# Attention scores from a doubled high query and stacked high and low keys, with unread transfers and transposes added at the end

## The chip, the core and the metric

The kernel runs on one core of a Trainium2 chip. The core has a matrix engine (TensorE, PE in the profile, with its weight loads as PEld), three engines for elementwise work (VectorE is DVE, ScalarE is ACT, GpSimd is POOL) and a sync engine (SP) that issues most transfers. The metric is the device time of one execution in microseconds (us). The kernel before took 609.4 us, the median of three runs (609.2 to 609.53).

## The reference

Two layers of a decoder trunk work on x of 256 x 1024 float32. In each layer one normalised input goes through one wide projection (9808 columns); three causal attentions of 8 heads of 64 read their queries, keys and values from it:

```
h = rms_norm(x, gain)
proj = einsum('bsd,de->bse', h, w_in)
oa = moba_attention(rope(qa), rope(ka), va) * silu(ga)     # mixer a
ob = dsa_attention(rope(qb), rope(kb), vb, qi, ki, wi) * silu(gb)   # mixer b
oc = forgetting_attention(qc, kc, vc, log_f) * silu(gc)    # mixer c
y = einsum('nbsw,nwd->bsnd', stack([oa, ob, oc]), w_branch)
x + einsum('bsd,de->bse', sum(sigmoid(merge) * y), w_out)
```

With 256 positions mixer a is plain causal attention (one block). Mixer b keeps, for each query, 64 keys by an index score: the weighted sum over 8 index heads of relu(qi . ki), with one key shared by the 8 heads. A last rms_norm follows the two layers.

## The kernel before

All products of float32 numbers on PE are made from split operands. ScalarE writes a high part in the matmul's own format (float32r), VectorE writes the low part as the difference, and a product is the sum of three matmuls: high by high, low by high, high by low. For weights this is `piece` (high on L362, low on L366); the activations `hTh` and `hTl` are split once a layer.

A unit is one output tile of the input projection: 24 matmuls with 256 moving columns for 128 output channels (`unit_b`, recorded at L410 in `mm_ops`), into one of three PSUM tiles called `proj`. Two heads of a mixer make a pair, and a pair is a unit each for query, gate and key. A query of mixer a or b is rotated (`rope`: VectorE, GpSimd, VectorE, GpSimd) and split into `qh` and `ql` by `split_to` (L396 and L397); a query of mixer c is split straight from PSUM (L400 and L401). A key is written by `write_bd` into a pair of tiles `bd..h` and `bd..l` of two blocks each: block 0 has head 0 in partitions 0 to 63, block 1 has head 1 in partitions 64 to 127, and the rest was set to zero at the start. So one matmul over 128 partitions with 2n moving columns gives n scores of each of the two heads, their columns alternating. `scores` (L584 to L586) issues six matmuls: for queries 0 to 127 against 128 keys three of 256 columns into `s0`, for queries 128 to 255 against 256 keys three of 512 columns into `s1`. Each has its own weight load, since the query part is the stationary operand.

`attend` goes on from there: VectorE adds mask or bias and takes the extreme (L647), ScalarE takes the exponential (L651), PE transposes the normalised rows (L673), the result is split again and multiplied with the values (L690 to L693, two of these with 128 moving columns), and `gated` multiplies with the gate. `index_scores` does query, scores, relu (L792, L793) and the weighted sum `isc` (L801, L803) for the four pairs of index heads; its key is written once a layer by `ev_kwf`, the same rows into both blocks.

A layer calls `scores` 16 times: four index pairs, and four pairs each of mixers a, c and b, in this order. Between them stand the merge gates (`unit_m`) and the branch projections (`unit_y`), interleaved by `between`; after mixer b come the rest of them and the output projection, two row tiles by two halves (and for the last layer the last tile in two column parts). `final_part` and `final_norm` then scale a row tile into `tmp6` and send it out, 384 columns by ScalarE's queue (L570) and 640 by SP's (L571).

The order of the instructions on each engine is fixed when the program is built: every operation is handed to a planner with its engine, an assumed duration, what it reads and writes, and a key. The planner simulates the engines and takes, on the engine that can start next, the operation with the smallest key. An operation marked `port` isn't planned on VectorE while one is planned on GpSimd. On the chip each engine runs its list in order and waits on semaphores.

Of the kernel before, what the change touches and what calls it, by code (L numbers as in the profile page):

```python
# [15 lines left out]
S = 256  # L16
# [31 lines left out]
NB1 = 0  # L48
# [186 lines left out]
def hybrid_trunk(ctx, tc, x, norm_gain, w_in, forget_bias, w_branch, w_out, final_gain, consts, out):  # L235
# [46 lines left out]
    qs = [[pool.tile([128, S], F32R, name=f"q{p}{i}") for i in range(3)] for p in "hl"]  # L282
# [8 lines left out]
    bd = [[pool.tile([128, 2, S], F32R, name=f"bd{i}{p}") for p in "hl"] for i in range(NBD)]  # L291
# [41 lines left out]
    for nm, n, cols, dt in (("rsh", 2, S, F32), ("rr", 2, S, F32),  # L333
                            ("th", 2, S, F32), ("g", 4, S, F32), ("e", 4, 384, F32), ("st", 8, 8, F32),
                            ("fb", 2, 384, F32), ("ot", 2, S, F32), ("t8", 4, 8, F32), ("mth", MTH, S, F32)):
        tag(nm, n, [128, cols], dt)
# [134 lines left out]
    def new_bd():  # L471

        b = Buf("bd")
        return b, [[Tok(), Tok()], [Tok(), Tok()]]


# [97 lines left out]
    def scores(q, k, ktoks, key):  # L574
        s0, s1 = Buf("s"), Buf("s")
        kt = [t for h in ktoks for t in h]

        def go():
            qh, ql = T(q[0]), T(q[1])
            kh, kl = T(k)  # L580
            for o, sl, n in ((T(s0)[:, :256], slice(0, 128), 128), (T(s1), slice(128, 256), 256)):
                o = o.rearrange("p (c h) -> p c h", h=2)
                mh, ml = (x[:, :, :n].rearrange("p h c -> p c h") for x in (kh, kl))
                PE.matmul(o, qh[:, sl], mh, start=True, stop=False)  # L584
                PE.matmul(o, ql[:, sl], mh, start=False, stop=False)  # L585
                PE.matmul(o, qh[:, sl], ml, start=False, stop=True)  # L586
        pe(go, 3 * (t_mm(256) + t_mm(512)), [q[0], q[1], k] + kt, [s0, s1], key, "qk", MARGIN)
        return s0, s1

    class Pair:  # L590
# [3 lines left out]
        def ev_q(self, ps, key):  # L594
            q = self.q = (Buf("qh"), Buf("ql"))
            if self.mixer == "c":
                split_to(lambda: plain(T(q[0])), lambda: plain(T(q[1])), lambda: tiles(T(ps)[:, :S]), S, True, [ps], q[0], q[1],
                         key, -0.125, "q")
            else:
                r = rope(ps, "q", key)  # L600
                split_to(lambda: plain(T(q[0])), lambda: plain(T(q[1])), lambda: tiles(T(r)), S, False, [r], q[0], q[1], key, name="q")

        def ev_k(self, ps, key):
            self.k, self.kt = new_bd()
            src = ps if self.mixer == "c" else rope(ps, "k", key)
            write_bd(src, self.k, self.kt, key, self.mixer == "c")
# [30 lines left out]
        def attend(self, key):  # L637
            bs = [self.bias(h, key) for h in range(2)]
            s0, s1 = scores(self.q, self.k, self.kt, key)
            es, ke = [], []  # L640
            for h in range(2):
# [4 lines left out]
                for t, a, n, s in parts:  # L646
                    dve(lambda t=t, a=a, n=n, s=s, e=e, st=st, b=b, h=h: DVE.tensor_tensor_reduce(  # L647
                        T(e)[:, a:a + n], T(s)[:, :2 * n].rearrange("p (c h) -> p h c", h=2)[:, h], b()[:, a:a + n], 1.0, 3e38, ALU.add, ALU.min,
# [72 lines left out]
    def write_bd(src, b, toks, key, ps, shared=False):  # L721
        for h in range(2):
            o = slice(64 * h, 64 * h + 64)
            s = (lambda: tiles(T(src)[0:64, :S])) if shared else (lambda o=o: tiles(T(src)[o, :S]))
            hi = lambda o=o, h=h: plain(T(b)[0][o, h])
            lo = lambda o=o, h=h: plain(T(b)[1][o, h])
            act(lambda hi=hi, s=s: ACT.activation(hi(), s(), AF.Copy), S, ps, [src, k_bdz], [toks[h][0]], key, "bd", HALF + (0.0 if ps else 104.0), touch=[b])
            dve(lambda hi=hi, lo=lo, s=s: DVE.tensor_tensor(lo(), s(), hi().bitcast(F32), op=ALU.subtract), S,
                [src, toks[h][0]], [toks[h][1]], key, "bd", t_dve(S) + HALF + 15.0, touch=[b], port=not ps)


    def ev_kwf(l, ps, key):
        act(lambda: ACT.activation(plain(wf[64:80]), tiles(T(ps)[64:80, :S]), AF.Copy), S, True, [ps], [k_wf], key, "wf")
        b, toks = new_bd()
        write_bd(rope(ps, "k", key, 64), b, toks, key, False, shared=True)
        return b, toks
# [357 lines left out]
```

## Time and profile before

| | before |
|---|---|
| median of three runs | 609.4 us |
| profiled execution, its own time | 609.16 us |
| its span in the profile | 607.4 us |
| PE busy | 599.1 us (99%) |
| PEld busy | 580.8 us (96%) |
| DVE busy | 537.9 us (89%) |
| ACT busy | 406.8 us (67%) |
| POOL busy | 85.7 us (14%) |
| bytes moved | 105.55 MB, mean 174 GB/s |

The time of an execution holds the span of the profile and what lies around it, here 609.16 - 607.4 = 1.76 us. Matmuls are pipelined, so a busy PE says only that matmuls follow one another; the pitch of their starts tells what one costs. L12 in a row is line 12 of the kernel; `out<-in` names the tiles an instruction writes and reads.

### The profile page before, as it was taken

Reading aid. Unit: us, or ns where it says so; the run is one execution under the profiler, and the core shown is the slowest. Engines: PE = TensorE matmul, PEld = TensorE weight load, DVE = VectorE, ACT = ScalarE, POOL = GpSimd, SP = SyncE. Lnnn points to the kernel's source line nnn. Section 1 sums busy time; section 2 is a strip of 40 time slices with the busy share of each in tenths; the row PEclk is TensorE's granted clock in tenths of the full one; section 3 lists DMA queues with packets and bytes.
Section 4 is the critical chain, followed back from the end, with each engine's and each line's share of the span. In section 5 each row is a group of like instructions: output and inputs, shape, how many; then the busy total and the mean of one; then the engine's idle time right before and its main releaser. Section 6 shows DMA issues by size and latency. Waiting matters only on the chain.

```text
span 607.4 us, 12561 instructions
## 1 busy us (share of the span) xinstructions
PE 599.1 (99%) x4856; PEld 580.8 (96%) x4856; DVE 537.9 (89%) x1270; ACT 406.8 (67%) x811; POOL 85.7 (14%) x100
## 2 busy tenths in 40 slices
PE   9999999999999999999999999999999999999995
PEld 8999999999999999999889999999999999999995
DVE  8799999887998999999588899978889989999883
ACT  6775487685776766785587554957767675859741
POOL 1224021100000222200003311201000004230001
PEclk9999999999999999999999999999999999999998
DMA  9866455837372562666555637474464437355801
GB/s 304 255 209 208 127 169 157 278 104 231 117 245 70 159 203 92 209 211 206 161 181 169 206 102 246 139 219 142 153 187 174 141 115 224 109 182 164 280 35 70
DMA packets 93853, 105.55 MB, mean 174 GB/s; under 512 B 4321, under 2 KB 82401, under 8 KB 93793
## 3 DMA queue, kind: packets, MB, share of 16 engines
q1 hardware_dynamic: 93504, 104.36, 53.8%
q8 instruction: 38, 0.62, 0.4%
q10 hardware_dynamic: 288, 0.39, 0.2%
q14 instruction: 23, 0.18, 0.1%
HBM read 103.69 MB, written 1.05 MB: 172 GB/s over the span
## 4 chain that ended last, share of the span: by engine, by line
PE 88%; DVE 9%; issue 1%; ACT 1%; DMA 0%; POOL 0%; POOLq 0%; DVEq 0%
PE proj L410 74%; DVE wl L366 3%; PE t L673 3%; PE proj L970 2%; PE s L586 2%; PE s L585 2%; PE s L584 2%; PE o L690 1%; PE o L693 1%; DVE isc L824 1%; DVE t L823 1%; PE t L629 1%; DVE isc L803 1%; DVE rsh L465 1%; PE o L692 0%
## 5 line engine op out<-in xcount | busy, mean ns | idle before, releaser
L366 DVE TENSOR_TENSOR wl<-raw,wh 128x1024 fp32r<-128x1024 f32 (+1 forms) x190 | 237.1, 1257 | 24.2 <-ACT wh L362 22.6
L362 ACT ACTIVATE wh<-raw 128x1024 fp32r<-128x1024 f32 (+1 forms) x190 | 198.6, 1058 | 74.3 <-PE proj L410 43.1
L410 PE MATMUL proj<-hTh,wh 128*128 128x256 f32 (+1 forms) x1040 | 246.4, 276 | 0.0
L410 PE MATMUL proj<-hTl,wh 128*128 128x256 f32 (+1 forms) x1040 | 245.6, 275 | 0.0
L410 PEld LDWEIGHTS proj<-hTl,wh 128*128 128x128 f32 (+1 forms) x1040 | 199.0, 191 | 0.4
L410 PEld LDWEIGHTS proj<-hTh,wh 128*128 128x128 f32 (+1 forms) x1040 | 198.9, 191 | 0.4
L410 PE MATMUL proj<-hTh,wl 128*128 128x256 f32 (+1 forms) x1040 | 160.1, 276 | 0.0
L410 PEld LDWEIGHTS proj<-hTh,wl 128*128 128x128 f32 (+1 forms) x1040 | 138.0, 191 | 0.9
L466 POOL TENSOR_TENSOR rsh<-rsh,cst 128x256 f32<-128x256 f32 (+1 forms) x42 | 33.0, 786 | 343.0 <-DVE rsh L465 333.9
L651 ACT ACTIVATE e<-e,st 128x128 f32<-128x128 f32 x96 | 42.6, 446 | 9.2 <-DVE st L647 8.9
L468 POOL TENSOR_TENSOR rr<-rr,rsh 128x256 f32<-128x256 f32 (+1 forms) x42 | 44.4, 1059 | 9.7 <-ACT wh L362 3.4
L410 PE MATMUL proj<-wh,v 128*128 128x512 f32 (+1 forms) x144 | 33.7, 356 | 0.0
L410 PE MATMUL proj<-og0l,wh 128*128 128x256 f32 x128 | 31.9, 275 | 0.0
L410 PE MATMUL proj<-og0h,wh 128*128 128x256 f32 x128 | 31.9, 275 | 0.0
L410 PE MATMUL proj<-wh,hTh 128*128 128x512 f32 x80 | 31.4, 393 | 0.0
L410 PE MATMUL proj<-wh,hTl 128*128 128x512 f32 x80 | 30.5, 382 | 0.2 <-DVE hTl L532 0.2
L706 ACT ACTIVATE ot<-o 64x256 f32<-64x256 f32 x48 | 18.3, 381 | 16.8 <-PE o L693 16.3
L410 PEld LDWEIGHTS proj<-wh,v 128*128 128x128 f32 x144 | 25.2, 190 | 2.9
L678 DVE TENSOR_TENSOR ptl<-t,pth 128x384 fp32r<-128x384 f32 x48 | 25.1, 551 | 0.2
L410 PE MATMUL proj<-og0h,wl 128*128 128x256 f32 x128 | 24.7, 275 | 0.0
L410 PEld LDWEIGHTS proj<-og0h,wh 128*128 128x128 f32 x128 | 24.6, 192 | 0.0
L410 PEld LDWEIGHTS proj<-og0l,wh 128*128 128x128 f32 x128 | 24.6, 192 | 0.0
(194 smaller groups left out, 1012.3 us busy)
## 6 DMA issues: line engine op xcount, KB each, us to landing
raw<-in_w_in_dram SPq DMA_DIRECT2D x74, 1024.0 KB, 5.2
raw<-in_w_branch_dram SPq DMA_DIRECT2D x24, 512.0 KB, 3.9
raw<-in_w_out_dram SPq DMA_DIRECT2D x8, 1024.0 KB, 5.5
raw<-in_w_in_dram SPq DMA_DIRECT2D x3, 512.0 KB, 6.3
x<-in_x_dram SPq DMA_DIRECT2D x4, 256.0 KB, 4.1
raw<-in_w_in_dram SPq DMA_DIRECT2D x2, 320.0 KB, 6.7
out_dram<-tmp SPq DMA_DIRECT2D x2, 320.0 KB, 2.5
raw<-in_w_in_dram SPq DMA_DIRECT2D x2, 256.0 KB, 3.4
```

Of the source, the lines that this page charges most:

```text
L362: ACT.activation(p[0].v, sel(c.v), AF.Copy)
L366: DVE.tensor_tensor(p[1].v, sel(c.v), p[0].v.bitcast(F32), op=ALU.subtract)
L410: PE.matmul(o(), a(), b(), start=first and i == 0, stop=last and i == n - 1)
L466: gps(lambda: POOL.tensor_tensor(T(sh)[:np_], T(sh)[:np_], s[:np_], op=ALU.mult), S, [k_rope], [sh], key, "rope")
L468: gps(lambda: POOL.tensor_tensor(T(r)[:np_], T(r)[:np_], T(sh)[:np_], op=ALU.add), S, [sh], [r], key, "rope")
L584: PE.matmul(o, qh[:, sl], mh, start=True, stop=False)
L585: PE.matmul(o, ql[:, sl], mh, start=False, stop=False)
L586: PE.matmul(o, qh[:, sl], ml, start=False, stop=True)
L651: act(lambda t=t, a=a, n=n, e=e, st=st: ACT.activation(T(e)[:, a:a + n], T(e)[:, a:a + n], AF.Exp, bias=T(st)[:, t:t + 1], scale=-1.0, acc ...
L673: PE.transpose(T(ps)[:, i * 128:(i + 1) * 128], T(es[h])[:, i * 128:(i + 1) * 128], ident)
L678: dve(lambda h=h, src=src: DVE.tensor_tensor(T(pl)[:, h], src(), T(ph)[:, h].bitcast(F32), op=ALU.subtract), 384, [ps, kp[h][0]], [kp[h][1 ...
L706: act(lambda r=r, h=h: ACT.activation(T(t)[r], T(o)[64:, h * S:(h + 1) * S], AF.Copy, scale=0.5), S, True, [o], [kt[h]], key, "og", HALF, ...
```

## The change

`scores` issues six matmuls of other sizes. The high query tile has two blocks: block h holds head h's rows in both halves of the partitions. A second key tile (`ke`, in place of the low key tile) holds in block h the high key of head h in one half of the partitions and its low key in the other. A matmul of `qh` block h with `ke` block h thus gives high by high plus high by low for head h, with n moving columns. One matmul of `ql` with the key tile of before (2n columns, zeros in it) gives low by high for both heads. `s1` is done ahead of `s0`, and the scores of the two heads stand one after the other and no longer alternate; the readers (L647, relu, `isc`) follow.

A query is now written by `split_q`: one ScalarE copy of 2 x 256 columns (both blocks), a ScalarE copy of 64 partitions into the lower half of block 1, VectorE's subtraction, and a ScalarE copy of 64 partitions into the upper half of block 0, which comes after the subtraction has read that tile. A key is written by `split_k`: one ScalarE copy of 2 x 256 columns, VectorE's two subtractions into the other halves, and two ScalarE copies of 64 partitions into the tile with zeros. The index key needs one subtraction in place of two, and three copies. Half of the key tiles no longer need to be set to zero. `qh` is twice as large and there is one more buffer `rr`; the scratch of GpSimd's transfers is set to 4096 bytes. `NB1` moves two merge gate units of mixer b from after it into it.

At the end of the last layer GpSimd issues four accumulating transfers of 512 KB each into a tile that nothing reads any more (`more`), once the first merged tile is there. `forms` adds one small ScalarE copy and 20 transposes on PE, which wait for the last writers of `tmp6` and whose results nothing reads. Branches under `Q_DMA` and `BD_DMA`, both False, aren't built.

```diff
-NB1 = 0
+NB1 = 2
+Q_DMA = False
+BD_DMA = False
...
-    qs = [[pool.tile([128, S], F32R, name=f"q{p}{i}") for i in range(3)] for p in "hl"]
+    qs = [[pool.tile([128, 2, S] if p == "h" else [128, S], F32R, name=f"q{p}{i}") for i in range(3)] for p in "hl"]
...
-    bd = [[pool.tile([128, 2, S], F32R, name=f"bd{i}{p}") for p in "hl"] for i in range(NBD)]
+    bd = [[pool.tile([128, 2, S], F32R, name=f"bd{i}{p}") for p in "he"] for i in range(NBD)]
...
-            kh, kl = T(k)
-            for o, sl, n in ((T(s0)[:, :256], slice(0, 128), 128), (T(s1), slice(128, 256), 256)):
-                o = o.rearrange("p (c h) -> p c h", h=2)
-                mh, ml = (x[:, :, :n].rearrange("p h c -> p c h") for x in (kh, kl))
-                PE.matmul(o, qh[:, sl], mh, start=True, stop=False)
-                PE.matmul(o, ql[:, sl], mh, start=False, stop=False)
-                PE.matmul(o, qh[:, sl], ml, start=False, stop=True)
+            kh, ke = T(k)
+            for o, sl, n in ((T(s1), slice(128, 256), 256), (T(s0)[:, :256], slice(0, 128), 128)):
+                both = kh[:, :, :n].rearrange("p h (a b) -> p h b a", a=2)
+                PE.matmul(o.rearrange("p (h b a) -> p h b a", h=2, a=2), ql[:, sl], both, start=True, stop=False,
+                          skip_group_check=True)
+                for h in range(2):
+                    oh = o[:, h * n:(h + 1) * n].rearrange("p (b a) -> p b a", a=2)
+                    PE.matmul(oh, qh[:, h, sl], turns(ke[:, 0 if shared else h, :n]), start=False, stop=True,
+                              skip_group_check=True)
...
+    def split_q(q, src, ps, b, key, scale, name):
...
+            act(lambda: ACT.activation(T(q[0]).rearrange("p h (a b) -> p h a b", a=2), two(src()), AF.Copy, **sc), 2 * S, ps,
+                [b], k[:2], key, name, 0.0 if ps else 144.0, touch=[q[0]])
+            hi = [(slice(0, 128), lambda: plain(T(q[0])[:, 0]).bitcast(F32), k[:1])]
+            act(lambda: ACT.activation(plain(T(q[0])[lo, 1]), src()[up], AF.Copy, **sc), S, ps,
+                [b], k[1:2], key, name, HALF + (0.0 if ps else 104.0), touch=[q[0]])
...
+                f = lambda r=r, hv=hv: DVE.tensor_tensor(plain(T(q[1])[r]), src()[r], hv(), op=ALU.subtract)
...
+            act(lambda: ACT.activation(plain(T(q[0])[up, 0]), src()[lo], AF.Copy, **sc), S, ps,
+                [b], k[:1], key, name, HALF + (0.0 if ps else 104.0), touch=[q[0]])
...
+    def split_k(src, ps, key):
...
+        act(lambda: ACT.activation(T(b)[1].rearrange("p h (a b) -> p h a b", a=2),
+                                   sv().unsqueeze(1).to_broadcast([128, 2, 2, 128]), AF.Copy), 2 * S, ps,
+            [src], [ka], key, "bd", 0.0 if ps else 144.0, touch=[b])
+        for h, (o, q) in enumerate(((LO, UP), (UP, LO))):
+            dve(lambda h=h, o=o, q=q: DVE.tensor_tensor(plain(T(b)[1][q, h]), tiles(T(src)[o, :S]), plain(T(b)[1][o, h]).bitcast(F32), op=ALU.subtract), S,
+                [src, ka], [kb[h]], key, "bd", t_dve(S) + HALF + 15.0, touch=[b], port=not ps)
...
+            for h, o in enumerate((LO, UP)):
+                act(lambda h=h, o=o: ACT.activation(plain(T(b)[0][o, h]), tiles(T(src)[o, :S]), AF.Copy), S, ps, [src, k_bdz], [k0[h]], key, "bd",
+                    HALF + (0.0 if ps else 104.0), touch=[b])
...
-                rr = rel[t].rearrange("p (c h) -> p h c", h=2)[:, h]
+                rr = rel[t][:, h * n:(h + 1) * n]
...
+            da, db = (og[1][p].rearrange("p k c -> p (k c)") for p in (1, 0))
+            src = w_in[l][:, :256].rearrange("(k p) c -> p k c", p=128)[:, :4]
+            def more():
+                for d, a in ((da, db.bitcast(F32)), (da, db.bitcast(F32)), (og[1][1], src), (og[1][1], src)):
+                    nc.gpsimd.dma_start(d, a, accum_op=ALU.add)
+            plan.op([("POOL", 4000.0, more)], k_og[1][0] + k_V[0][0], k_og[1][1], units[0], 5000.0, "more")
...
+            for a, i, o in ((tmp6, ident, None), (tmp6, turns(ident), 2), (hTh, idr, None), (hTh, turns(idr), 2), (tmp6, ident, 3)):
+                for r in range(4):
...
+                    PE.matmul(d, src, i, is_transpose=True, start=True, stop=True)
...
+        pe(emit, 4000.0, [k_main, k_idr] + k_tmp + hT_all[0], b, 10 ** 6, "forms")
...
-    nc = _bacc.Bacc("TRN2", target_bir_lowering=False, num_devices=1)
+    nc = _bacc.Bacc("TRN2", target_bir_lowering=False, num_devices=1, dynamic_dma_scratch_size=4096)
```

More of the change, by code (lines that the diff above doesn't have):

```diff
@@ L47 @@
 HI_KEY = (-60, -48, -47, -46)
-NB1 = 0
+NB1 = 2
+Q_DMA = False
+BD_DMA = False
+FULL = False
 BANKS = ("proj", "s", "t", "o")
@@ L571, in final_norm, with move, go, scores @@
         plan.op([("SP", 50.0, lambda: nc.sync.dma_start(out_rows[:, B], tmp6[:, B]))], [ko[1], k_tmp[1]], [], key, 1900.0, "out")
-    def scores(q, k, ktoks, key):
+    def move(dst, src, n, reads, writes, key, name, touch=()):
+        def go():
+            for d, a in zip(dst(), src()):
+                nc.sync.dma_start(d.bitcast(F32), a.bitcast(F32))
+        o = plan.op([("SP", 1250.0, go)], reads, writes, key, 1900.0, name, touch)
+        o.margin = -1350.0
+    def scores(q, k, ktoks, key, shared=False):
@@ L638, in attend @@
             bs = [self.bias(h, key) for h in range(2)]
-            s0, s1 = scores(self.q, self.k, self.kt, key)
+            s0, s1 = scores(self.q, self.k, self.kt + self.qt, key)
             es, ke = [], []
@@ L719, in gated @@
                      k_og[self.oi][0][self.p], k_og[self.oi][1][self.p], key, name="og")
[L721 to L729, printed above, removed]
+    LO, UP = slice(0, 64), slice(64, 128)
@@ L732, in ev_kwf @@
     def ev_kwf(l, ps, key):
         act(lambda: ACT.activation(plain(wf[64:80]), tiles(T(ps)[64:80, :S]), AF.Copy), S, True, [ps], [k_wf], key, "wf")
-        b, toks = new_bd()
-        write_bd(rope(ps, "k", key, 64), b, toks, key, False, shared=True)
-        return b, toks
+        r, b = rope(ps, "k", key, 64), Buf("bd")
+        ka, k0, k1 = Tok(), Tok(), Tok()
+        sv = lambda: tiles(T(r)[LO, :S])
+        for o, h, k in ((LO, 0, k0), (UP, 1, k1)):
+            act(lambda o=o, h=h: ACT.activation(plain(T(b)[0][o, h]), sv(), AF.Copy), S, False, [r, k_bdz], [k], key, "bd",
+                HALF + 104.0, touch=[b])
@@ L738, in wf_cols @@
+        act(lambda: ACT.activation(plain(T(b)[1][LO, 0]), sv(), AF.Copy), S, False, [r], [ka], key, "bd", HALF + 104.0, touch=[b])
+        dve(lambda: DVE.tensor_tensor(plain(T(b)[1][UP, 0]), sv(), plain(T(b)[1][LO, 0]).bitcast(F32), op=ALU.subtract), S,
+            [r], [ka], key, "bd", t_dve(S) + HALF + 15.0, touch=[b], port=True)
+        return b, [ka, k0, k1]
     def wf_cols(l, key):
@@ L912, in hybrid_trunk @@
     for b in bd:
-        for t in b:
+        for t in b[:1]:
             z = t.rearrange("p h c -> p (h c)")
```

76 lines of the change are left out of this document (60 added, 16 removed).

## The prediction, made before the result was known

> **What bounds the kernel now.** I read the page first: busy times, then the chain.
>
> ```profile
> span 607.4 us, 12561 instructions
> ...
> PE 599.1 (99%) x4856; PEld 580.8 (96%) x4856; DVE 537.9 (89%) x1270; ACT 406.8 (67%) x811; POOL 85.7 (14%) x100
> ...
> PE 88%; DVE 9%; issue 1%; ACT 1%; DMA 0%; POOL 0%; POOLq 0%; DVEq 0%
> ```
>
> PE is busy 599.1 of 607.4 us, and the chain runs through PE for 88% and through VectorE for 9%. A busy PE need not be an efficient one, so the next view is the windows, cut by stage, with the count of matmuls beside the time (columns: stretch, its length, then busy us and count of PE, PEld, DVE, ACT, POOL, clock, DMA share, GB/s).
>
> ```profile
> 37.00:90.00 53.00, 52.89 (x457) 52.17 (x456) 51.34 (x140) 33.00 (x61) 10.80 (x12) 1.00 0.56 177
> 90.00:135.00 45.00, 45.00 (x358) 43.20 (x357) 40.20 (x90) 33.97 (x72) 6.80 (x9) 1.00 0.57 181
> 201.00:268.00 67.00, 67.00 (x600) 66.63 (x599) 64.42 (x152) 48.16 (x104) 15.70 (x17) 1.00 0.52 162
> 345.00:382.00 37.00, 36.49 (x322) 36.14 (x321) 35.88 (x102) 19.98 (x35) 5.94 (x8) 1.00 0.57 174
> 498.00:565.00 67.00, 67.00 (x600) 66.63 (x598) 63.79 (x151) 48.46 (x103) 16.69 (x17) 1.00 0.53 163
> ```
>
> From 201 to 268 us 600 matmuls take 67.00 us, 0.112 us each. From 37 to 90 it is 53.00 / 457 = 0.116, with some matmuls of 512 columns among them. So PE streams without a gap there, and whatever shortens PE's own work shortens the kernel, unless another engine is next. The one that is near is VectorE: 51.34 of 53, 64.42 of 67, 35.88 of 37 and 63.79 of 67 us in four of the windows, 96% on average. ScalarE has room everywhere (at most 33.97 of 45 here).
>
> **The change part by part.** *The matmuls of `scores`.* The timeline of PE around one call:
>
> ```profile
> 545.53 0.28 PE L584 MATMUL s<-bd0h,qh 128*128 128x256 f32 x1
> ...
> 545.87 0.38 PE L584 MATMUL s<-bd0h,qh 128*128 128x512 f32 x1
> ...
> 546.52 0.61 PE L410 MATMUL proj<-hTh,wl 128*128 128x256 f32 x4
> ```
>
> From start to start a call takes 546.52 - 545.53 = 0.99 us: three of 256 columns in 0.34 (0.112 each, as in the windows) and three of 512 in 0.65 (0.217 each). Now it is one of 512, three of 256 and two of 128. What does one of 128 columns cost? Two places say different things. First the product with the values, whose L691 and L692 have 128 columns, and the weight loads beside them; then a place with 8 columns and full weights:
>
> ```profile
> 564.34 0.22 PE L691 MATMUL o<-pth,v 128*128 128x128 f32 x1
> 564.40 0.22 PE L692 MATMUL o<-ptl,v 128*64 128x128 f32 x1
> ...
> 564.35 0.14 PEld L692 LDWEIGHTS o<-ptl,v 128*64 128x64 f32 x1
> ```
>
> ```profile
> 37.46 0.37 PE L778 MATMUL t<-fz,cst 128*128 128x8 f32 x2
> 37.68 0.37 PE L779 MATMUL t<-fz,ones 128*128 128x8 f32 x2
> 37.91 0.36 PE L584 MATMUL s<-bd0h,qh 128*128 128x256 f32 x1
> ```
>
> L691 and L692 start 0.06 us apart, but the load that runs under L691, the one for L692, has only 64 columns (0.14 us long). With loads of 128 columns even matmuls of 8 columns go at (37.91 - 37.46) / 4 = 0.11 us. The load of the next weights runs under the current matmul, and a full load needs about 0.11 us. Both short matmuls of the new `scores` are followed by a full load (the next `qh` block, then whatever comes next), so I take 0.112 for them, with 0.06 as the low end. A call is then 0.217 + 5 x 0.112 = 0.777 us, a gain of 0.213; the low end is 0.673, a gain of 0.317. The count of calls is in the windows with the tile `qh` alone (PE's count is four matmuls per call):
>
> ```profile
> 37.00:90.00 53.00, 6.71 (x24) 4.11 (x24) 2.97 (x6) 1.96 (x4) 1.00 0.56 177
> 201.00:268.00 67.00, 4.38 (x16) 2.74 (x16) 1.97 (x4) 1.89 (x4) 1.00 0.52 162
> 345.00:382.00 37.00, 2.35 (x8) 1.36 (x8) 1.31 (x3) 1.03 (x3) 1.00 0.57 174
> 498.00:565.00 67.00, 4.38 (x16) 2.74 (x16) 1.86 (x4) 1.87 (x4) 1.00 0.53 163
> ```
>
> There are 16 calls a layer, 32 in all, so PE gets 32 x 0.213 = **6.8 us** shorter (10.1 at the low price).
>
> [...]
>
> *ScalarE's copies.* The groups by form give every kind:
>
> ```profile
> L396 ACT ACTIVATE qh<-rr 128x256 fp32r<-128x256 f32 x24 | 11.5, 480 | 0.2 <-POOL rr L468 0.2
> L727 ACT ACTIVATE bd0h<-rr 64x256 fp32r<-64x256 f32 x12 | 5.8, 484 | 1.3 <-POOL rr L468 1.2
> L793 ACT ACTIVATE tmp<-s 128x512 f32<-128x512 f32 x8 | 4.7, 593 | 0.5 <-PE s L586 0.5
> L482 ACT ACTIVATE tmp<-x 128x512 f32<-128x512 f32 x6 | 3.8, 657 | 4.6 <-DVE x L1059 4.6
> L400 ACT ACTIVATE qh<-proj 128x256 fp32r<-128x256 f32 x8 | 3.0, 377 | 2.1 <-PE proj L410 2.0
> L727 ACT ACTIVATE bd0h<-proj 64x256 fp32r<-64x256 f32 x6 | 2.3, 379 | 1.9 <-PE proj L410 1.8
> ```
>
> A rotated query had one copy of 480 ns; it gets one of 512 columns (657 ns, the nearest row) and two of 484, 1.15 us more; 24 of them make 27.5 us. A query of mixer c: 593 - 377 + 2 x 379 = 0.97 us more, 8 of them 7.8. A key gets one copy more: 16 x 0.657 + 8 x 0.593 = 15.3. The index key 2 x 0.484 = 1.0. ScalarE goes from 406.8 to about 458 us, 76% of the span. In the window where it is fullest, 90 to 135, four pairs would add 4 x 1.8 = 7.2 to 33.97 of 45. This lies beside PE and I cost it at nothing by itself. If that cover were gone, it is the chain that pays: a key reaches `scores` 0.6 to 0.66 us later, since the 512 copy stands ahead of the others.
>
> *VectorE* does as many subtractions for pairs as before, one less for each index key and six clears less at the start. The reads of `isc` become contiguous; no row shows what that is worth, between nothing and a little relief. All of it is in favour and I count none of it. But in the four windows where VectorE is at 96%, 6 + 4 + 2 + 4 = 16 calls give PE 16 x 0.213 = 3.4 us, while VectorE's idle time there is 1.66 + 2.58 + 1.12 + 3.21 = 8.6 us. So the gain fits, but with less play for a fixed order. New waits of PE: between 0 and 3.4 us; I take **0.8**, a quarter, since VectorE keeps over half of its idle time. A gain below zero I leave out, as PE waits hardly at all today. The longer chains into `scores`, the extra `rr` buffer and the moved gate units go into the same number: they reorder work that PE has to do anyway.
>
> *The transposes at the end.* They wait for `tmp6`, which ScalarE's row below finishes. The timeline, the waits of SP, windows on the clock, and two lines on what a matmul of 128 columns costs cold and warm:
>
> ```profile
> 600.77 0.39 PE L410 MATMUL proj<-wl,v 128*128 128x256 f32 x2
> ...
> 603.06 0.61 ACT L566 ACTIVATE tmp<-x,fsum 128x384 f32<-128x384 f32 x1 [3.51 <-POOL fsum L561]
> 603.71 0.35 ACTq L570 DMA_DIRECT2D out_dram<-tmp  x1
> ...
> SPq L1090 <- DMA out_dram<-tmp: 2.3, 1, 2.3
> ...
> 603.00:604.00 1.00, 0.00 (x0) 0.00 (x0) 0.55 (x1) 0.61 (x1) 0.03 (x1) 0.60 0.00 0
> 604.00:607.00 3.00, 0.00 (x0) 0.00 (x0) 0.00 (x0) 0.00 (x0) 0.00 (x0) 0.50 0.47 175
> ...
> 1.05 5.67 PE L885 MATMUL t<-ones 128*128 128x128 f32 x28 [1.05 <-DVE ones L881]
> 455.39 0.66 PE t L673 x6
> ```
>
> PE's last product ends at 601.16, `tmp6` is written at 603.67 and its transfer issued until 604.06. SP then waits 2.3 us for the outputs, from about 604.06 to 606.36, and the span ends 1.05 us after that. Transposes that start near 603.85 take 20 x 0.11 = 2.2 us at the pace of L673 (0.66 / 6) and end, with the pipeline's 0.3, at 606.35: just hidden. But the granted clock has fallen to 0.50 by 604. The cold start shows that pace: 5.67 / 28 = 0.20 us for each matmul of 128 columns. Then they take 20 x 0.20 = 4.0 us and end near 608.2, 1.85 us after the outputs. Between 0 and 1.9 I take **1.6**, nearly the cold price, as eight of the twenty are float32r and may be shorter.
>
> [...]
>
> *The four unread transfers.* Nothing reads their tile. They start when the first merged tile is there, and are over before the outputs if these rows bound them:
>
> ```profile
> 573.05 0.91 ACT L400 ACTIVATE v<-acc 128x256 fp32r<-128x256 f32 x2
> raw<-in_w_branch_dram SPq DMA_DIRECT2D x24, 512.0 KB, 3.9
> raw<-in_w_in_dram SPq DMA_DIRECT2D x3, 512.0 KB, 6.3
> 597.56 0.93 POOL L561 TENSOR_TENSOR fsum<-fsum,half 128x1 f32<-128x1 f32 x1 [53.79 <-DVE fsum L559]
> ```
>
> A transfer of 512 KB lands in 3.9 to 6.3 us; four in a row take 16 to 25 us and end at 591 to 600. GpSimd's next work is the root at 597.56. Should it be held until 600, the first row tile goes out 2.4 us later and the second, which reuses `tmp6`, about 1.1. Between 0 and 1.1 I take **0.2**. Weights that share the transfer engines with them fall under the same bounds.
>
> *Sum*, on the profiled execution's own 609.16: - 6.8 + 0.8 + 1.6 + 0.2 = -4.2, so 604.96. The median of the runs is 0.24 above that execution: **605.2 us**.
>
> **The rivals.** *The short matmuls go at 0.06 us* (as L691 does): 10.1 in place of 6.8, 605.2 - 3.3 = 601.9. Against it stand the 8-column rows. *The transposes are hidden* (the clock still full when they start): 605.2 - 1.6 = 603.6. For it: at the pace of L673 they would end with the outputs. *VectorE is the bound in its four full windows*: all 3.4 us are lost there in place of 0.8, 605.2 + 2.6 = 607.8. For it: 96%; against it: its own work doesn't grow. *Slower than before: PE waits for the split.* A key's 512 copy, 0.66 us, lies on the way to `scores`, and a query's last copy must wait for VectorE's subtraction with ScalarE's queue (exponentials, weight splits) behind it. If PE had to wait the full 0.66 at each of 24 pairs it would be 15.8, at half of that 7.9: 605.2 - 0.8 + 7.9 = 612.3. It decides the sign from 4.2 / 24 = 0.18 us a pair on. Against it: the list of PE's waits holds hardly a score today:
>
> ```profile
> PE s L586 <- DVE bd2l L728: 0.5, 1, 0.5
> ```
>
> **How the numbers follow.** The forecast 0.52, short matmuls 0.08, hidden transposes 0.15, VectorE 0.17, slower 0.08. A measurement of this kernel tells about 0.2% from no change, 1.2 us, so faster means below 608.2. The forecast, the first two rivals and half of VectorE's case lie there: 0.83. Same 0.10, slower 0.07. The range leaves out the far end of the short matmuls and the slower case: 602.2 to 608.6.
>
> **What would show it.** Pitch of the two 128-column matmuls, 0.11 or 0.06 us; a call of `scores` from start to start near 0.78; ScalarE near 458 us; VectorE unchanged; PE's windows with as few gaps as before; the 20 transposes after `tmp6` at 0.20 us each and the end of the span after them, not after the outputs. I am wrong if PE shows new waits for `qh` or the key tiles, or if GpSimd's root for the first row tile comes late.

## The result, and the profile after

The changed kernel takes 617.7 us (median of four runs, 616.52 to 618.56) against 609.46 for the kernel before in the same job: a ratio of 1.0133, interval 1.0112 to 1.0155. Forecast were 605.2 us and a gain. The change costs 8.2 us. The four executions of the changed kernel differ in the mean clock that PE was granted: two of 616.5 and 616.9 us at a mean clock of 0.997 and two of 618.5 and 618.6 at 0.994 and 0.992, and the profiled one is the fastest. The page of the changed kernel, with the lines quoted of before and the one on the clock:

```profile
span 614.7 us, 12635 instructions
...
PE 599.0 (97%) x4876; PEld 579.8 (94%) x4876; DVE 541.6 (88%) x1268; ACT 458.4 (75%) x897; POOL 87.8 (14%) x103
...
PEclk9999999999999999999999999999999999999899
...
PE 66%; DVE 21%; ACT 6%; DMA 4%; issue 2%; SPq 0%; POOL 0%; POOLq 0%; DVEq 0%; ACTq 0%
```

ScalarE's 458.4 us is what was forecast, VectorE's work has hardly grown (541.6 us against 537.9), and PE is busy as long as before although its matmuls are shorter. The chain that ended last now runs through PE for 66% instead of 88%, and through VectorE, ScalarE and transfers for the rest. One call of `scores` in the timeline:

```profile
519.64 0.38 PE L587 MATMUL s<-bd1h,ql 128*128 128x512 f32 x1
519.86 0.38 PE L591 MATMUL s<-bd1e,qh 128*128 128x256 f32 x2
520.08 0.28 PE L587 MATMUL s<-bd1h,ql 128*128 128x256 f32 x1
520.19 0.33 PE L591 MATMUL s<-bd1e,qh 128*128 128x128 f32 x2
520.36 0.66 PE L413 MATMUL proj<-hTh,wl 128*128 128x256 f32 x4
```

From start to start it takes 520.36 - 519.64 = 0.72 us, 0.721 as the median of the 32 calls, where it was 0.985. So PE's own work is 32 x 0.264 = 8.4 us shorter, more than the 6.8 forecast. The two matmuls of 128 columns together take 520.36 - 520.19 = 0.17 us: in the records the first goes at 0.058, the second at 0.112.

So 8.4 us were won and 16.6 lost. The list of PE's waits in the changed kernel (total us, times, longest) shows places that it did not have before:

```profile
PE proj L413 <- ACT og0h L399: 5.6, 2, 4.3
PE s L1148 <- ACT tmp L563: 2.6, 1, 2.6
PE proj L413 <- DVE bd0e L766: 1.6, 2, 0.9
...
PE proj L413 <- DVE bd1e L766: 0.9, 1, 0.9
...
PE proj L413 <- DVE bd2e L766: 0.6, 1, 0.6
```

Hardly any wait is at `scores` itself. The longest stands ahead of a branch projection that needs the last pair of mixer b (`og0h`, written by ScalarE on L399). The three lines on L766 (four waits) are units of mixer c that find no free `proj` tile, because VectorE still reads a key from one. The one on L1148 is before the transposes at the end, where nothing waits for PE any more.

To compare the kernels, each matmul's time from its start to the next one's start is set against what its form takes unhindered (0.218 us for 512 columns, 0.112 for 256, 0.058 for a short one followed by its like), and the excess is summed by stage from the records of the profiled runs. a, c, b are the mixers (a with the index), y the branch projections after mixer b, o the output projection; the two layers follow one another. Small negative numbers mean that a form's price is some ns too high. "Plan" is the PE idle time that the kernel's own planner counted when it made the order: its estimate, no measurement. For e9 it is that of before, made for the matmuls of before. The table leaves out the first and the last microseconds of a run. e8's profiled execution took 612.0 us, 2.5 above its median; a stretch at half clock in it is 1.7 of that. Some expectations below give e2's loss as 10.4 and e8's as 11.5 us; the table's 12.2 and 13.3 stand in their place.

```
us lost by PE       a     c     b     y     o  |  a     c     b     y     o  |  sum   plan
before            1.7  -0.2  -0.3  -0.1   0.0  | 1.6  -0.2  -0.3  -0.1  -0.1 |  2.2   2.0
after             3.8   2.0   0.2   2.0   0.0  | 1.6   2.0   0.3   6.3  -0.1 | 18.0
e1 plan only      3.0   2.1   0.2   2.1   0.0  | 1.6   2.0   0.2   1.5  -0.1 | 12.4
e2 no unread      2.9   2.0   0.2   1.7   0.0  | 1.6   2.0   0.2   1.7  -0.1 | 12.2   7.3
e3 NB1 = 0        3.5   2.0   3.0  -0.1   0.0  | 1.6   2.0   3.0  -0.1   0.0 | 14.8   9.0
e5 matmuls        4.2   0.9   0.4   5.1   0.0  | 1.5   0.9   0.4   5.2  -0.1 | 18.6  12.7
e6 copies         3.1   2.5   0.5   0.4   0.0  | 0.4   2.5   0.3   0.4  -0.1 | 10.1   6.5
e7 prices         3.4   1.1   0.8   6.4   0.0  | 1.6   1.0   0.7   3.7  -0.1 | 18.6  12.3
e8 mixer c        3.6   1.1   0.9   0.8   0.0  | 1.6   1.3   0.4   3.7  -0.1 | 13.3   5.0
e9 old order      3.1   0.5   0.5  -0.1   0.0  | 2.3   0.5   0.0  -0.1  -0.1 |  6.9   2.0
e10 new order     3.1   1.0   0.9  -0.1   0.0  | 1.3   0.8   0.9  -0.1  -0.1 |  7.8   2.2
e13 no halves     2.8   2.0   0.2   1.9   0.0  | 1.4   2.0   0.2   1.9  -0.1 | 12.3   7.3
e14 prices too    2.3   0.2   2.3  -0.1   0.0  | 1.2   0.1   2.2  -0.1  -0.1 |  8.1   2.1
```

### The profile page after: what moved, and what is told of

It reads as the page before. It is cut to its first block, busy times and chain, and to the rows that moved or that the text cites. A ratio compares the mean times of both kernels' runs of the same rounds, so it can differ in the third digit from the quotient of the medians.

```text
span 614.7 us, 12635 instructions
## 1 busy us (share of the span) xinstructions
PE 599.0 (97%) x4876; PEld 579.8 (94%) x4876; DVE 541.6 (88%) x1268; ACT 458.4 (75%) x897; POOL 87.8 (14%) x103
## 4 chain that ended last, share of the span: by engine, by line
PE 66%; DVE 21%; ACT 6%; DMA 4%; issue 2%; SPq 0%; POOL 0%; POOLq 0%; DVEq 0%; ACTq 0%
PE proj L413 57%; DVE wl L369 8%; DMA raw<-in_w_out_dram 3%; ACT wh L365 3%; DVE e L682 2%; PE t L708 2%; PE proj L1024 1%; DVE isc L878 1%; PE s L591 1%; DVE t L877 1%; DMA x<-in_x_dram 1%; PE s L587 1%; DVE bd0e L766 1%; DVE bd2e L766 1%; ACT e L686 1%
## 5 line engine op out<-in xcount | busy, mean ns | idle before, releaser
L365 ACT ACTIVATE wh<-raw 128x1024 fp32r<-128x1024 f32 (+1 forms) x190 | 197.4, 1054 | 48.0 <-PE proj L413 31.2
L686 ACT ACTIVATE e<-e,st 128x128 f32<-128x128 f32 x96 | 42.6, 444 | 11.2 <-DVE st L682 10.9
L471 POOL TENSOR_TENSOR rr<-rr,rsh 128x256 f32<-128x256 f32 (+1 forms) x42 | 41.8, 995 | 14.4 <-DVE rr L470 7.4
L413 PE MATMUL proj<-og0h,wh 128*128 128x256 f32 x128 | 33.4, 285 | 5.6 <-ACT og0h L399 5.6
L711 ACT ACTIVATE pth<-t 128x384 fp32r<-128x384 f32 x48 | 22.1, 488 | 5.4 <-PE t L708 5.3
```

What stands on the lines that cost most here:

```text
L365: ACT.activation(p[0].v, sel(c.v), AF.Copy)
L413: PE.matmul(o(), a(), b(), start=first and i == 0, stop=last and i == n - 1)
L471: gps(lambda: POOL.tensor_tensor(T(r)[:np_], T(r)[:np_], T(sh)[:np_], op=ALU.add), S, [sh], [r], key, "rope")
L686: act(lambda t=t, a=a, n=n, e=e, st=st: ACT.activation(T(e)[:, a:a + n], T(e)[:, a:a + n], AF.Exp, bias=T(st)[:, t:t + 1], scale=-1.0, acc ...
L711: act(lambda h=h, src=src: ACT.activation(T(ph)[:, h], src(), AF.Copy), 384, True, [ps], [kp[h][0]], key, "pT", touch=[ph])
```

## The experiments

### The unread transfers and transposes

**e1** plans the transfers as the change does but issues none, so the order of everything else is the changed kernel's. **e2** has neither transfers nor transposes.

```diff
 e1: def more():
-        for d, a in ((da, db.bitcast(F32)), ...): nc.gpsimd.dma_start(d, a, accum_op=ALU.add)
+        pass
 e2:
-    plan.op([("POOL", 4000.0, more)], ..., "more")
-    forms()
```

> The changed kernel with the four unread transfers planned as before (so the order on every engine is the same) but none of them issued; it leaves out work that nothing reads. Theory 'transfers': beside the loads of the output weights they make ScalarE wait for weights with a needed copy of the last pair queued behind, 5 to 6 us of PE's time between 565 and 580 us; without them 611.5 to 612.5 us. Rival 'order': the order that the plan makes around GpSimd's booked 4 us is the cause, not the traffic; then 617 to 618 as the changed kernel. Rival 'splits': the extra copies of the split are the whole loss and the traffic is hidden; also 617 to 618.

> The changed kernel without the unread transfers and without the transposes at the end. 'transfers': 611.5 to 612.5, the same as with the transfers planned but not issued, since the transposes ended before the outputs landed in the profile (613.3 against 613.4 us). 'order': also about 612. 'splits': 617 to 618. If the transposes cost what was forecast, this run is 1.6 us below the one that only drops the transfers.

e1 took 611.51 us (ratio 1.0037, 1.0019 to 1.0055), e2 611.5 (1.0029, 1.0019 to 1.0039). So on the medians, whose intervals are about 1 us wide to either side, the transposes cost nothing and the transfers cost 617.7 - 611.5 = 6.2 us (18.0 - 12.4 = 5.6 us in the table of the profiled executions). The trace of the changed kernel says how. First the timeline around the place, GpSimd, PE and ScalarE:

```profile
550.18 1.04 POOL L1105 DMA_DIRECT2D og1l<-og1h  x1
556.00 0.89 POOL L1105 DMA_DIRECT2D og1l<-og1h  x1 [4.78 <-DMA og1l<-og1h]
...
563.13 1.32 POOL L1105 DMA_DIRECT2D og1l<-in_w_in_dram  x1 [6.24 <-DMA og1l<-og1h]
575.37 1.29 POOL L1105 DMA_DIRECT2D og1l<-in_w_in_dram  x1 [10.92 <-DMA og1l<-in_w_in_dram]
...
571.18 0.28 PE L413 MATMUL proj<-og0l,wh 128*128 128x256 f32 x1
575.79 0.58 PE L413 MATMUL proj<-og0h,wh 128*128 128x256 f32 x1 [4.34 <-ACT og0h L399]
...
573.41 2.00 ACT L365 ACTIVATE wh<-raw 128x1024 fp32r<-128x1024 f32 x2 [3.83 <-DMA raw<-in_w_out_dram]
575.32 0.42 ACT L399 ACTIVATE og0h<-ot 128x256 fp32r<-128x256 f32 x1
```

The first transfer starts at 550.18, inside mixer b, and not when the first merged tile is there (578.22): the transfers don't read that tile, so the planned dependence brings no wait on the chip. GpSimd issues it directly behind its last `rr` step, half a microsecond after PE's last read of `og1`. The four run one behind the other, and the third is issued at 563.13, beside the first load of `w_out` (563.06). ScalarE, which works in order, stands 3.83 us before such a piece of `w_out` (L365), and the copy `og0h` that PE needs is queued behind it. In e1, in the same order, that piece waits little and `og0h` is done at 572.42:

```profile
570.08 2.01 ACT L365 ACTIVATE wh<-raw 128x1024 fp32r<-128x1024 f32 x2 [0.36 <-DMA raw<-in_w_out_dram]
572.00 0.42 ACT L399 ACTIVATE og0h<-ot 128x256 fp32r<-128x256 f32 x1
```

The load that ScalarE stands before is a piece of the chain that ended last in both runs, in the changed kernel first, then in e1:

```profile
563.06 10.33 DMA raw<-in_w_out_dram
```

```profile
563.20 6.86 DMA raw<-in_w_out_dram
```

The stall has a second price. The windows of the changed kernel (columns as in the prediction):

```profile
572.26:575.67 3.41, 0.00 (x0) 0.00 (x0) 1.17 (x1) 2.26 (x3) 0.30 (x1) 1.00 1.07 375
575.67:579.08 3.41, 3.29 (x14) 3.12 (x15) 2.43 (x5) 0.89 (x3) 0.99 (x1) 0.50 0.89 254
579.08:582.49 3.41, 3.41 (x32) 3.41 (x32) 1.78 (x5) 1.97 (x3) 0.00 (x0) 1.00 1.14 279
```

After the empty stretch PE got half its clock for 3.41 us and started 14 matmuls instead of some 30, which is 1.7 us more.

**e4** is the kernel before with the same transfers and transposes added, nothing else. **e12** is the changed kernel with only the first two transfers, those from SBUF.

```diff
 e12:
-    for d, a in ((da, db.bitcast(F32)), (da, db.bitcast(F32)), (og[1][1], src), (og[1][1], src)):
+    for d, a in ((da, db.bitcast(F32)), (da, db.bitcast(F32))):
```

> The kernel before with the unread transfers, the transposes and the small scratch added and nothing else changed. 'transfers': the same loads are met, 612 to 615 us. If the traffic only hurts together with the late last pair of the changed kernel: 609.4 to 610.5. The transposes alone as forecast (half clock, after the outputs): 611.0; hidden: 609.4.

> The changed kernel in its own order, with only the first two of its four unread transfers issued (SBUF to SBUF; the two that read w_in from DRAM are left out). In the changed kernel the four ran from 550 to about 585 us, one behind the other, and the w_out loads from 563 on took 8.0 us instead of 5.5. Theory 'meeting': the price is that the transfers meet the w_out loads; the two end at about 563, so 611.5 as without any (range 611 to 612.5), without a half clock at 575. Rival 'queue': GpSimd standing at its transfers, or the SBUF traffic, delays the last pair of mixer b, whatever the loads do: the first two hold GpSimd 4.8 and 6.2 us, so 614 to 618.

e4 took 611.1 us (1.0025, 1.0016 to 1.0035): 1.7 us in the order of before, where the third transfer starts at 559.67 us and no wait for `og0h` stands in the list. e12 took 611.08 (1.003, 1.0018 to 1.0042), no more than e1 without any, although GpSimd waits 4.7 us for the first transfer there too. So 'queue' falls, and the price belongs to the two transfers from DRAM, which stand beside the `w_out` loads, as 'meeting' has it. That they slow the load (10.33 us against 6.86 in e1) by sharing the way with it is my reading of the two traces, not tried by a run of its own. The transfers in its list (KB each, median us to landing):

```profile
og1l<-og1h POOLq DMA_DIRECT2D x2, 512.0 KB, 6.2
og1l<-in_w_in_dram POOLq DMA_DIRECT2D x2, 512.0 KB, 9.3
```

### What is left of the loss without them

611.5 us is still 10.5 above 609.4 - 8.4 = 601.0. Five kernels ask which part of the change does it.

**e3** is e2 with `NB1 = 0`, as before. **e5** is e2 with the splits of the kernel before, so of the work only the matmuls are new (the operands are not stacked, the scores not the reference's); it is planned anew. **e6** is the reverse: the new copies, and matmuls of the sizes of before (scores not the reference's either). **e7** is e2 with the wide copies planned at their measured 0.79 and 0.60 us. **e8** is e2 with mixer c's q and k first copied out of PSUM by one ScalarE copy, which frees the `proj` tile sooner.

```diff
 e3:
-NB1 = 2
+NB1 = 0
 e7 (three places):
-  0.0 if ps else 144.0
+  122.0 if ps else 264.0
 e8:
-  self.qt = split_q(q, lambda: tiles(T(ps)[:, :S]), True, ps, key, -0.125, "q")
+  r = stage(ps, key, -0.125)
+  self.qt = split_q(q, lambda: tiles(T(r)), False, r, key, None, "q")
...
+  def stage(ps, key, scale):
+      r = Buf("rr")
+      act(lambda: ACT.activation(T(r), T(ps)[:, :S], AF.Copy, scale=scale), S, True, [ps], [r], key, "stage")
```

> As the run without the unread work, with the two merge gate units of mixer b back behind it (NB1 = 0). If moving them took away the work that PE had while the last pair of mixer b was finished (stalls of 1.4 and 4.5 us before the branch projections in the two layers), this is 1 to 2 us faster than the run with NB1 = 2, about 610.5; if the stalls come from the splits alone, the same within 0.5 us.

> No unread work; the new six matmuls of each scores call (one wide, two half-wide for each query tile), but queries and keys are written as in the kernel before (one copy of 256 columns for a query, two half copies for a key). The high query is not doubled and high and low keys do not stand in one block, so the scores are not the reference's; only the time counts. Theory 'splits' (the matmuls do save 0.213 us a call, and the extra copies and the order they bring eat it): 609.4 - 6.8 = 602.6, between 602 and 604. Rival 'no gain' (another engine sets the pace, so shorter matmuls bring nothing): 608.5 to 610.

> No unread work; queries and keys written as in the changed kernel, but scores uses matmuls of the sizes of before (three of 256 and three of 512 columns a call; the operands are not the right ones, so the result is not the reference's). 'splits' as a pure addition: the copies cost about 8.9 us in PE's waits beside either set of matmuls, 609.4 + 8.9 = 618.3. If the waits only appear because PE got faster (a bound by VectorE or ScalarE further on): 610 to 612, hardly more than the 611.5 of the run with both.

> As the run without unread work, but the plan books the wide copies of 512 columns at what the profile of the changed kernel shows (about 0.79 us from SBUF and 0.60 from PSUM, in place of 0.665 and 0.478). Theory 'plan': the waits come from an order made with copies 0.12 us too cheap, 56 of them; then most of the 8.9 us goes, 604 to 607. Rival 'chain': the copies themselves keep tiles and inputs late whatever the order: 610.5 to 612.5.

> As the run without unread work, but in mixer c queries and keys are first copied out of PSUM by one ScalarE copy of 256 columns, and all the splitting reads that copy, so the projection tile is free after about 0.4 us. Theory 'tile held': PE's waits of 1.1 and 0.8 us twice in mixer c (3.8 us) come from the projection tile that the split holds until VectorE's subtractions and ScalarE's last copy are done; without them 607.7 to 608.5. If that wait has another cause, no gain, or a little slower for the 16 extra copies: 611.5 to 613.

e3 took 613.5 us (1.0063, 1.0048 to 1.0078), e5 618.01 (1.0138, 1.0119 to 1.0158), e6 616.11 (1.0116, 1.0101 to 1.0131), e7 618.01 (1.0159, 1.0135 to 1.0183), e8 609.49 (1.001, 0.9997 to 1.0023). Taking the copies away made it 6.5 us slower, and so did truer prices: neither 'splits' nor 'plan prices' survives as I had put it. In the table the loss wanders: e3 loses nothing at y and 3.0 in each mixer b, e5 little in mixer c and over 5 at each y (1.7 of it half clock behind a wait of 3.0 us for `og0h`), e8 less in mixer c and more at the second y, where its profiled execution has the half clock. What the five have in common is that each was planned anew, and the planner's own count of PE's idle time was 5 to 13 us in each (2.0 in before). That gave the next theory: the order.

### The order

**e9** is the kernel before in its own order, with the same copies, splits and planned prices; only the six matmuls that a call emits are the new ones (scores not the reference's).

```diff
-            for o, sl, n in ((T(s0)[:, :256], slice(0, 128), 128), (T(s1), slice(128, 256), 256)):
-                o = o.rearrange("p (c h) -> p c h", h=2)
-                mh, ml = (x[:, :, :n].rearrange("p h c -> p c h") for x in (kh, kl))
-                PE.matmul(o, qh[:, sl], mh, start=True, stop=False)
...
+            for o, sl, n in ((T(s1), slice(128, 256), 256), (T(s0)[:, :256], slice(0, 128), 128)):
...
+                    PE.matmul(oh, qh[:, sl], turns(kl[:, h, :n]), start=False, stop=True,
```

> The kernel before, in its own order to the instruction (copies, splits, planned prices and filler units as they were), with only the six matmuls of a scores call replaced by two of full and four of 128-column width as in the change. The operands are not stacked, so the scores are not the reference's; only their cost is looked at. Theory 'order': the matmul gain is whole and the loss comes from the new order in which the list scheduler puts the work once any price or instruction changes; here nothing moves, so 609.4 - 32 x 0.209 = 602.7, range 602 to 604, PE's loss in all stages about 2.2 us as before. Rival 'form': the new matmuls themselves (their sizes, their order, both halves of one PSUM tile) let PE wait; run e5 had them with the splits of before and took 618.0. Then 607 or more, and PE's loss is 6 us or more in the mixers.

605.77 us (0.994, 0.9925 to 0.9954). Against e5, which has the same matmuls and the same kinds of splits, the order (with `NB1` and the buffers that it was planned for) is worth 618.0 - 605.8 = 12.2 us, of which e5's two stretches at half clock are 3.4. But 605.8 is not the 602 to 604 expected, and by the 8.4 us that the calls really save it should be 601.0. 4.7 us are lost although nothing was moved. The windows from the end of one mixer to the end of the next, before:

```profile
135.32:200.97 65.65, 65.65 (x542) 63.78 (x541) 57.43 (x137) 44.77 (x98) 0.00 (x0) 1.00 0.51 161
200.97:267.87 66.90, 66.90 (x599) 66.53 (x598) 64.32 (x152) 48.06 (x104) 15.70 (x17) 1.00 0.52 162
```

and the same work in e9, with three lines of the waits of its weight loads:

```profile
134.56:199.92 65.36, 65.33 (x543) 63.37 (x542) 57.77 (x138) 45.14 (x98) 0.00 (x0) 1.00 0.52 165
199.92:266.53 66.61, 66.56 (x599) 65.99 (x598) 64.05 (x152) 47.84 (x104) 15.71 (x17) 1.00 0.51 161
```

```profile
PEld t L675 <- DVE e L663: 1.2, 3, 0.6
...
PEld s L583 <- DVE ql L397: 0.8, 1, 0.8
PEld s L587 <- DVE bd2l L730: 0.7, 2, 0.4
```

Each of these stages has four calls, 1.06 us less work, and became 0.29 us shorter. PE comes earlier to a transposition, to `scores` or to a unit and finds VectorE not done. Between 30 and 590 us the waits in the list of the weight loads grow from 2.3 us in before to 4.6, 1.9 of it for VectorE and 0.4 for ScalarE. That is half of the 4.7; that the rest is more of the same, in waits too short for the list, is argued and not shown stage by stage. In mixer c the list has one:

```profile
PEld t L631 <- DVE ptl L680: 0.3, 1, 0.3
```

The new call also does `s1` ahead of `s0` and needs `ql` first. The swap is not the loss: of the 24 calls of `attend` VectorE's first read of the scores waits for the matmuls in two, 0.11 us each. In mixer b VectorE is busy 64.05 of 66.61 us; in mixer c only 57.77 of 65.36, so there it is not full; its single steps stand where the old order put them.

**e10** has the whole change but for the unread work, with mixer c's copy of e8, `NB1 = 0` and a planned safety distance of 250 ns, chosen because the planner counts only 2.2 us of PE idle time there. **e11** adds the unread transfers and transposes to it.

```diff
-MARGIN = 200.0
+MARGIN = 250.0
-NB1 = 2
+NB1 = 0
```

> e8 (the change without unread transfers and transposes, mixer c's q and k copied out of PSUM first by one ScalarE copy each) with no m unit held back in mixer b (NB1 = 0) and the planned safety distance ahead of PE's scores and transposes 250 instead of 200 ns: the same arithmetic and the same kinds of instructions as e8, in another order, picked because the planner's own estimate of PE's idle time is 2.2 us there against 5.0 in e8 and 7.3 in e2 (1.96 in the kernel before). Theory 'order': PE's loss falls from 10.4 (e2) and 11.5 (e8) to 3 to 4.5 us and the time to 603 to 606, below the kernel before. Rival 'copies': the wide copies and the extra half copies have a price that PE must wait for in any order; the c and y stages keep 4 us or more of loss and the time stays at 608.5 to 613.

> e10 with the four unread transfers and the 20 unread transposes of the change. If the transfers cost what they did in e1 against after (6.2 us: ScalarE stands at a w_out piece, PE stalls over 3 us and falls to half clock), e10 + 5 to 7. If their price hangs on how near the last pair of mixer b is to the first w_out pieces, as e4 has it (1.7 us with the kernel before), e10 + 0.5 to 3; with NB1 = 0 the m units stand between the two, as they do in before, so I expect this one.

e10 took 606.3 us (0.9951, 0.9936 to 0.9965): 3.1 us below the kernel before and 5.2 below e2, although ScalarE has more work than in the changed kernel. Its page:

```profile
span 604.5 us, 12578 instructions
...
PE 595.1 (98%) x4856; PEld 576.3 (95%) x4856; DVE 537.5 (89%) x1267; ACT 468.1 (77%) x913; POOL 89.4 (15%) x99
```

e11 took 610.13 (1.001, 1.0 to 1.0019): the unread work costs 3.8 us here. I expected 0.5 to 3. Of it 3.2 us are lost in the output projection, behind weight splits and the merged tile:

```profile
PE proj L413 <- DVE wl L369: 1.7, 3, 1.3
...
PE proj L413 <- ACT v L403: 0.7, 1, 0.7
```

**e13** keeps e2's order and only leaves out ScalarE's half-width copies of each q and k (scores not the reference's). **e14** is e10 planned on other prices, so once more the same instructions in another order.

```diff
 e13 (three places):
-  act(lambda: ACT.activation(plain(T(q[0])[lo, 1]), src()[up], AF.Copy, **sc), S, ps,
+  act(lambda: None, S, ps,
 e14:
-  ("DVE", "PE"): 200.0     MARGIN = 250.0     SPLIT_LEAD = 2.0     0.0 if ps else 144.0
+  ("DVE", "PE"): 250.0     MARGIN = 275.0     SPLIT_LEAD = 3.0     122.0 if ps else 264.0
```

> e2 (the change without unread transfers and transposes) in its own order, with the half-width ScalarE copies of each pair's q and k left out (for q the two that set the heads apart, for k the two into the tile with zeros; they stay in the plan at their price but emit nothing, so the scores are not the reference's). ScalarE loses 32 x 2 x 0.4 + 24 x 2 x 0.4 = some 45 us and is down at the 407 to 415 us of the kernel before. Theory 'order': PE still finds its units in e2's order, whose waits were in the plan already; its loss stays at 8 us or more of 10.4 and the time at 609 to 611.5. Rival 'copies': ScalarE was late with the copies; the waits of mixer c (1.8 us each) and of the branch stage (1.7 each) go, the loss falls to 5 or less and the time to 604 to 606.

> e10 with its plan made on other prices: the wide copies at their measured 0.79 and 0.60 us, VectorE's score step 20 ns and its hand-over to PE 50 ns dearer, safety distance 275 ns, weight splits one step earlier. The instructions are the same kinds and numbers, the order is another; the planner's own PE idle time is 2.1 us (e10 2.2). Theory 'order': an order with little planned idle time and truer prices keeps the gain: 603 to 606.5, PE's loss 3 to 6 us. Rival 'prices do not matter and planned idle time says little': 608 or more, as e7 (618.0) was with truer prices and 12.3 us of planned idle time.

e13 took 611.17 us (1.003, 1.0021 to 1.004), as e2, with ScalarE down from 458.3 to 409.4. Its list of PE's waits has the same places as e2's, two of them under the name of another last step (`e`, L686); e2 first, then e13:

```profile
PE proj L413 <- ACT og0h L399: 1.9, 2, 1.0
PE proj L413 <- DVE bd0e L766: 1.6, 2, 0.9
```

```profile
PE proj L413 <- ACT og0h L399: 2.2, 2, 1.1
PE proj L413 <- ACT e L686: 1.3, 2, 0.6
...
PE proj L413 <- DVE bd0e L766: 1.0, 1, 1.0
```

So the half copies are not the cause: 49 us of ScalarE's work less give nothing. e14 took 606.63 us (0.9954, 0.9939 to 0.9969), as e10 and against e7's 618.0 with truer prices. Its one large wait is in mixer b and not in c:

```profile
PE proj L413 <- DVE rr L470: 2.0, 2, 1.0
```

The planner's count is a fair guide: 2.0 to 2.2 us where PE lost 6.9 to 8.1 (e9, e10, e14), 5.0 to 6.5 where it lost 10.1 to 13.3 (e6, e8), 7.3 to 12.7 where it lost 12.2 to 18.6. It is no price, since even the good orders of the new matmuls lose 5 to 6 us more than it counts.

## Why the prediction was wrong

**The sum.** On the medians: 609.4 - 8.4 (shorter matmuls) + 4.7 (waits in the unchanged order, e9) + 5.7 (e2 against e9) + 0 (transposes) + 6.2 (transfers) = 617.6. Forecast were - 6.8, + 0.8 for all waits and new order together, + 1.6 and + 0.2.

**The matmuls: right, and a size off.** I took 0.112 for both short ones, with 0.06 as the low end; one goes at 0.058, so a call takes 0.721 and not 0.777. That a full load needs 0.11 us, as I had inferred, does not hold here: the second of the two loads 128 columns and starts 0.058 us after the first. The 8-column rows that decided it multiply `fz` by `cst`, plain float32 and not the float32r of `scores`: the nearest row by columns was not the nearest by type. The transposes at the end of the changed kernel, with 128 columns and full loads, show the same difference: those of float32 follow one another at 0.109 us or more, the last six of the eight of float32r at 0.082 to 0.086. The pair in `scores` takes 0.17 us, 0.085 each, where I had 0.112.

**New waits of PE: the step that failed first.** "I take 0.8 ... VectorE keeps over half of its idle time", bounds 0 to 3.4. e9 measured 4.7 with nothing moved. The bound came from the idle time of a whole window, as if VectorE's work could slide in it. In an order that is fixed, PE that arrives early at one of VectorE's steps waits for that step, also in mixer c, where VectorE has 7.6 us idle. The rival that let VectorE take all of the gain in the full windows was nearer than the forecast, and still too small.

**"... they reorder work that PE has to do anyway."** This held the largest error of thought. The longer chains, the extra buffer, the new prices and `NB1` gave the list scheduler another problem, and it returned an order that costs 5.7 us more than the old one (e2 against e9). The planner's own count had said so: 7.3 us of PE idle time in e2's order against 2.0 before, a figure that the prediction did not ask for. e13 shows that the half copies do not make it, e10 and e14 that other orders with all copies take back 5 us of the 5.7; e5 against e9 shows 12.2 us between two orders of nearly the same work, half clock included. That e8, e10 and e14 also empty mixer c's PSUM tiles sooner is part of their gain (in e8 mixer c's two losses fall from 4.0 to 2.4 us); how much of the 5.7 hangs on the wide copies reading PSUM in e2's own order was not tried.

**The unread transfers.** "They start when the first merged tile is there, and are over before the outputs": they start at 550.18 us, because the planned dependence brings no wait. So two of them stand beside the `w_out` loads, which I had not put on the list, and a late load holds ScalarE's queue with `og0h` behind it. 0.2 with a bound of 1.1 became 6.2, and 1.7 and 3.8 in other orders (e4, e11).

**The transposes at the end.** + 1.6 became 0 on the medians, and the reason is in part luck. The tail of the changed kernel:

```profile
610.37 0.62 ACT L563 ACTIVATE tmp<-x,fsum 128x384 f32<-128x384 f32 x1 [3.51 <-POOL fsum L558]
611.01 0.35 ACTq L567 DMA_DIRECT2D out_dram<-tmp  x1
...
611.03 1.20 PE L1148 MATMUL s<-cst,tmp 128*128 128x128 f32 x8 [2.57 <-ACT tmp L563]
...
612.70 0.60 PE L1148 MATMUL s<-cst,tmp 128*64 128x128 f32 x4
```

They run from 611.03 to 613.30 at the full clock, and the span ends 6.28 us after PE's last product, where it is 6.22 in e2 without them. In e1's profiled execution the clock fell to half at 606.74, as forecast:

```profile
606.38 1.67 PE L1147 MATMUL s<-cst,tmp 128*128 128x128 f32 x8 [2.56 <-ACT tmp L563]
...
608.81 1.06 PE L1147 MATMUL s<-cst,tmp 128*64 128x128 f32 x4
```

There they took until 609.87 and the span ended 6.88 us after PE's last product. So they cost 0.06 us in the execution with the full clock and 0.66 in the one with the half; the order of the rest was the same. The rival that hid them was right for the profiled execution; 1.6 was too much for either case.

**ScalarE** came out in size (458.4 against 458) and cost nothing by its busy time (e13). The sum was in part luck: the 40 wide copies from SBUF took 0.78 to 0.80 us in place of 0.657, some 5 us more, while among others fewer of the normalising steps fell to ScalarE (32 in place of 37). **Slower**, at 0.08, was the outcome, but not by its mechanism: PE does not wait at `scores` for the split, it waits for PSUM tiles and for the last pair.

## What to carry to other kernels

Where a program fixes the order of every engine, work taken from the bound engine may be a gain only up to the next step of another engine that the old order had placed to fit; here, with nothing moved, 3.7 of 8.4 us arrived. And any change to such a kernel's operations gives a new order, whose quality must be separated from the change itself: try the change in the old order, and try several orders of the new one, before judging it. Work that nothing reads still has a place in the queues, and here its price was set by what ran beside it: the first two alone, issued 13 and 7 us ahead of the first `w_out` load, cost nothing that the runs show (e12), all four 6.2, 1.7 and 3.8 us in three orders.

## What the runs showed of the hardware

Behind a wait of PE the changed kernel was granted half the clock for 3.41 us (575.67 to 579.08). In the traces of the kernel before and of the changed one the changes of the granted clock lie 3.41 us or a multiple of it apart: 570.03 us of full clock, which is 167 x 3.413, then 3.41 of half and 37.55, 11 x 3.413, of full in the changed one; 597.33 us of full clock, 175 x 3.413, in before. The stretch ahead of the half clock had no matmul in the changed kernel; in e8 one wait of 1.51 us left PE 1.81 of 3.41 us busy, and the next stretch was granted 0.50:

```profile
568.86:572.27 3.41, 1.81 (x14) 1.43 (x13) 2.69 (x4) 2.48 (x4) 0.00 (x0) 1.00 1.04 393
572.27:575.68 3.41, 3.41 (x19) 3.41 (x18) 2.33 (x7) 1.65 (x3) 0.00 (x0) 0.50 0.68 227
```

So this stall of 1.5 us cost 3.2. Not every stretch with a gap was followed by half the clock. Two more, one of before and one of the changed kernel, both at full clock:

```profile
599.78:603.20 3.42, 1.38 (x13) 1.19 (x11) 1.78 (x8) 0.14 (x1) 0.66 (x1) 1.00 0.41 153
```

```profile
606.39:609.80 3.41, 2.08 (x19) 1.89 (x17) 2.04 (x8) 0.46 (x3) 0.13 (x1) 1.00 0.41 154
```

Behind the first, with PE busy for 1.38 us, came the half clock (603.20), behind the second, with 2.08, the full one. These few cases give no rule for where the line lies. At the end of the kernel PE's clock fell 2.0 us after its last product in before, in e1 2.9 us after it (606.74), and in the changed kernel it was still full when the transposes started 2.6 us after it.

The accumulating transfers of 512 KB took 6.2 us from SBUF and 9.3 us from DRAM in the changed kernel, one at a time; a plain load of 512 KB of `w_branch` landed in 4.1 in the same run (median of 24). A ScalarE copy that reads 256 columns twice took 0.78 to 0.80 us from SBUF and 0.60 from PSUM, where the nearest contiguous copies of 512 columns had taken 0.66 and 0.59.
